# Windowed attention in pairs of blocks, with negated scores and four output tiles begun among the last ones

## The chip, the cores and the metric

The kernel runs on one core of a Trainium2 chip. The metric is the device time of one execution in microseconds (us). Before the change the median of three runs is 1871.75 us (1870.81 to 1874.26); the profile is of a further execution.

## The reference

An encoder of two layers on two sequences, a prompt of 256 rows and a sample of 512, with model width 1024, in fp32. Layer l=0 mixes rows by a gated recurrence (mLSTM), layer l=1 by windowed attention, and behind each mixer stands a gated FFN with a convolution of width 3. Only the attention is touched: 16 heads of 64 share 4 key/value heads; a block of 128 queries sees up to 384 keys (its own block and one on each side), and each head has a sink that counts in the denominator alone.

```python
s = jnp.einsum('bqkgd,bckd->bkgqc', qb, kb).astype(jnp.float32) * scale + bias
s = jnp.where(valid, s, -jnp.inf)
m = jnp.maximum(jnp.max(s, axis=-1, keepdims=True), sink_l)
p = jnp.exp(s - m)
denom = jnp.sum(p, axis=-1, keepdims=True) + jnp.exp(sink_l - m)
ob = jnp.einsum('bkgqc,bckd->bqkgd', p / denom, vb.astype(jnp.float32))
```

The result goes through an output projection, x = x + g1 * (ob @ w_out), and then into the FFN.

## The kernel before

Everything lies transposed, features on the 128 partitions and the 768 rows of both sequences along the free axis. A product of fp32 precision is made of three matmuls in a reduced format: each operand is split into a high part (a cast on ScalarE, `whi` or `zh`) and the rest (a subtraction on VectorE, `wlo` or `zl`), and PE computes hi by hi, lo by hi and hi by lo (L230). Weights come in loads of 512 KB into five buffers `raw`, and `split` puts them into `whi` and `wlo`, which rotate over three buffers each. An instruction that writes into a rotating buffer waits until the readers of its last content are done.

The attention is in `swa`. First keys and values are projected, then come the blocks: 8 head pairs j, for each the sample's four blocks and the prompt's two, 48 in all. `scores` makes for both heads e of the pair two matmuls into one of four PSUM banks `pa`, adds the bias and takes the maximum in one VectorE instruction (L1092), joins the sink by three small VectorE instructions (L1097 to L1099), takes the exponential with its row sum on ScalarE (L1101), that of the sink (L1104), adds, inverts (L1105, L1106) and scales on POOL (L1108). `flip` transposes the block on PE (L1116) and copies it out of PSUM, one head by ScalarE and one by VectorE. `values` multiplies by v into a bank `ps`, and behind a sequence's last block ScalarE copies the bank out (L1137); `pack` splits that once more for the projection. The query projections of the next head pairs are a generator, `project`, each of whose steps is three matmuls.

The order of PE is written out by hand (manual_schedule): per block a few steps of `project`, the scores of block x, the transposes of block x - 3, and after each third block the values of three blocks. Other engines run in the order in which their instructions are written, and so do the DMA issues on SP.

`out_proj` computes 16 tiles of 128 features by 384 rows, 24 matmuls each, and adds each to x on VectorE (L719, the residual). It is a generator over `tiles()`, which fetches and splits a tile's weights when it is advanced. It yields ahead of tile 8 and ahead of tile 15, the last. Between these yields `prepare` splits some of the FFN's first weights; what follows the second is `head`, which loads the four halves of the first FFN weights, writes the splits wa[0], the subtractions of `sums(0)` (L1390 to L1395 on VectorE) and the split wc[0], and only then runs the last tile. Then come the norm's row sums, the matmul on `nr`, the squared sum's power, which POOL works out, and the FFN's own products. For l=0 `prepare` splits three weights ahead, for l=1 one; the other two splits (128x1024) are in the head.

## Time and profile before

| what | us |
|---|---|
| median of three runs | 1871.75 |
| the profiled execution | 1875.08 |
| its span | 1873.0 |
| PE busy in the span | 1801.3 |
| VectorE busy | 1400.9 |
| attention blocks, first to last matmul | 1100.2 to 1257.8 |
| output projection of l=1 | 1257.8 to 1327.6 |

A busy time says only that an instruction was under way on the engine. The chain of waits and the timeline give in brackets for how long an engine was idle before an instruction, and whose end released it; the windows give busy times by stage, with the clock that was granted to PE.

### The profile page before, as it was taken

What the parts mean: (1) busy time and instruction counts of PE and PEld (TensorE: products, weight loads), DVE (VectorE), ACT (ScalarE), POOL (GpSimd) and SP (SyncE); (2) the same over time, 40 slices, a digit from 0 to 9 for tenths busy, and PEclk for the clock granted to TensorE, in tenths of its full rate; (3) what the DMA queues carried; (4) which work ended last, traced back from release to release, by engine and by line L of the source; (5) the groups of instructions that cost most, each with busy time, mean ns of one, the idle gap of its engine ahead of it and who ended that gap; (6) DMA issues with size and microseconds to landing.
All of it is one profiled execution on the core that took longest, in us unless ns stands there. A gap on an engine that the chain in (4) does not pass through costs nothing. (4 is left out here: it accounts for less than half of the span.)

```text
span 1873.0 us, 29153 instructions
## 1 busy us (share of the span) xinstructions
PE 1801.3 (96%) x11306; PEld 1662.3 (89%) x11306; DVE 1400.9 (75%) x2306; ACT 911.0 (49%) x1841; POOL 497.9 (27%) x390
## 2 busy tenths in 40 slices
PE   6989999999999999999999999989999999999997
PEld 5968887878988999999999898879989999999996
DVE  4866567685689777777777768875997777777777
ACT  4544334444455444444444556763565444444443
POOL 2011001031024333333331313330134333333322
PEclk9999999999999999999999999999999999999999
DMA  8353466555212222222222221212222222222211
GB/s 325 108 165 134 152 197 205 162 167 193 97 50 74 68 68 68 68 68 68 68 68 82 101 90 41 89 55 90 79 79 79 68 68 68 68 68 68 68 35 68
DMA packets 64246, 184.49 MB, mean 99 GB/s; under 512 B 6167, under 2 KB 23831, under 8 KB 64108
## 3 DMA queue, kind: packets, MB, share of 16 engines
q1 hardware_dynamic: 64108, 182.63, 30.1%
q8 instruction: 89, 1.46, 0.3%
q14 instruction: 49, 0.40, 0.1%
HBM read 176.17 MB, written 6.43 MB: 97 GB/s over the span
## 5 line engine op out<-in xcount | busy, mean ns | idle before, releaser
L236 ACT CAST whi<-raw 128x1024 fp32r<-128x1024 f32 x237 | 249.0, 1051 | 389.9 <-PE pa L230 198.6
L237 DVE TENSOR_TENSOR wlo<-raw,whi 128x1024 fp32r<-128x1024 f32 x237 | 316.3, 1335 | 108.8 <-ACT whi L236 107.7
L230 PE MATMUL pa<-slab,whi 128*128 128x256 f32 (+1 forms) x1472 | 346.9, 333 | 6.2 <-DVE slab L719 6.2
L230 PEld LDWEIGHTS pa<-slab,whi 128*128 128x128 f32 x1472 | 253.2, 190 | 33.1 <-DVE slab L719 7.1
L719 DVE SCALAR_TENSOR_TENSOR slab<-pa,mod,slab 128x256 f32<-128x256 f32 (+1 forms) x368 | 207.5, 591 | 70.9 <-PE pa L230 70.6
L230 PE MATMUL ps<-zh,whi 128*128 128x256 f32 (+2 forms) x688 | 233.4, 340 | 6.3 <-ACT whi L236 2.6
L230 PE MATMUL pa<-slab,wlo 128*128 128x256 f32 (+1 forms) x736 | 234.9, 331 | 0.0
L230 PE MATMUL ps<-zh,wlo 128*128 128x256 f32 (+2 forms) x688 | 228.3, 334 | 3.8 <-DVE wlo L237 3.8
L230 PE MATMUL ps<-zl,whi 128*128 128x256 f32 (+2 forms) x688 | 228.7, 334 | 1.4 <-DVE zl L539 0.9
L1275 PE MATMUL ps<-zh,whi 128*128 128x384 f32 x504 | 171.0, 339 | 6.4 <-ACT ps L1330 5.4
L1276 PE MATMUL ps<-zl,whi 128*128 128x384 f32 x504 | 169.7, 337 | 0.8 <-DVE zl L1233 0.8
L1277 PE MATMUL ps<-zh,wlo 128*128 128x384 f32 x504 | 169.0, 335 | 0.0
L230 PEld LDWEIGHTS pa<-slab,wlo 128*128 128x128 f32 x736 | 139.3, 190 | 12.9 <-DVE wlo L237 0.9
L230 PEld LDWEIGHTS ps<-zh,whi 128*128 128x128 f32 x688 | 132.2, 192 | 20.3 <-issue 3.5
L230 PEld LDWEIGHTS ps<-zh,wlo 128*128 128x128 f32 x688 | 132.2, 192 | 14.6 <-DVE wlo L237 4.6
L230 PEld LDWEIGHTS ps<-zl,whi 128*128 128x128 f32 x688 | 132.3, 192 | 10.7 <-DVE zl L539 1.1
L1531 POOL TENSOR_TENSOR slab<-slab 128x772 f32<-128x772 f32 x44 | 87.4, 1987 | 190.3 <-DVE slab L1503 178.9
L1306 POOL TENSOR_TENSOR raw<-raw,raw 128x512 f32<-128x512 f32 x40 | 53.7, 1341 | 291.7 <-DVE wlo L237 243.8
L1502 DVE SCALAR_TENSOR_TENSOR slab<-slab,cstt,slab 128x771 f32<-128x771 f32 x88 | 106.2, 1208 | 25.4 <-ACT slab L1500 25.4
L1503 DVE SCALAR_TENSOR_TENSOR slab<-slab,cstt,slab 128x771 f32<-128x771 f32 x88 | 120.1, 1365 | 0.8
L1303 POOL TENSOR_TENSOR raw<-raw 128x512 f32<-128x512 f32 x40 | 64.8, 1619 | 186.1 <-DMA raw<-in_w_dram 178.4
L472 DVE SCALAR_TENSOR_TENSOR ada<-raw,silc,ada 128x1024 f32<-128x1024 f32 x84 | 111.5, 1358 | 2.6 <-DMA raw<-in_adaln_w_dram 2.6
(300 smaller groups left out, 4163.8 us busy)
## 6 DMA issues: line engine op xcount, KB each, us to landing
raw<-in_w_dram SPq DMA_DIRECT2D x208, 512.0 KB, 3.7
raw<-in_adaln_w_dram SPq DMA_DIRECT2D x84, 512.0 KB, 4.5
slab<-in_x_dram SPq DMA_DIRECT2D x12, 512.0 KB, 7.7
slab<-in_adaln_w_dram SPq DMA_DIRECT2D x12, 512.0 KB, 10.3
slab<-mrows SPq DMA_DIRECT2D x8, 384.0 KB, 6.0
xs<-slab SPq DMA_DIRECT2D x6, 512.0 KB, 2.9
bt<-brow SPq DMA_DIRECT2D x16, 192.0 KB, 3.2
slab<-xs SPq DMA_DIRECT2D x6, 512.0 KB, 5.7
```

The lines of the kernel that those rows point to most:

```text
L230: self.last_mm = self.nc.tensor.matmul(out, lhsT, rhs, start=start, stop=stop)
L236: nc.scalar.copy(hi, src)
L237: return nc.vector.tensor_tensor(lo, src, hi.bitcast(F32), ALU.subtract)
L472: stt(acc[:, s], row, w, acc[:, s], ALU.mult, ALU.add)
L719: self.nc.vector.scalar_tensor_tensor(x, o, self.mod[l][:, gc + c, q : q + 1], x, ALU.mult, ALU.add)
L1275: mm(o, wh[:, k], hi[k], start=start and k == 0, stop=False, skip_group_check=True)
L1276: mm(o, wh[:, k], lo[k], start=False, stop=False, skip_group_check=True)
L1277: mm(o, wl[:, k], hi[k], start=False, stop=k == 3, skip_group_check=True)
L1303: tt(q[2], q[2], q[3], ALU.add)
L1502: stt(y[:, 1:], u[:, :-1], w(0), y[:, 1:], ALU.mult, ALU.add)
L1503: stt(y[:, :-1], u[:, 1:], w(2), y[:, :-1], ALU.mult, ALU.add)
L1531: nc.gpsimd.tensor_tensor(y, y, yrow[:, j], ALU.mult)
```

## The change

Scores are negated: queries are scaled by -0.125 and the bias changes sign, so that the minimum, begun at the negated sink, serves as the exponential's bias with a scale of -1. POOL copies the sink into the column behind the keys, so that the row sum holds it. Blocks go in 24 pairs. The transposes lag by one pair, and the values of three pairs, a whole head pair, come in one burst. Their result is split straight out of PSUM. For the last head pair the prompt's blocks come first. `out_proj` becomes the class `Out`: tiles 0 and 1 run six of their eight k steps among pairs 20 to 23, their seventh and tile 2 behind, then they are closed (residual and square), and the last value matmuls, tile 2 and tile 3 follow; `rest` does the other twelve. x is loaded when the last scores have been computed. `prepare` is the same for both layers.

```diff
-    def out_proj(self, u0, act, xt, l, apply):
-        def tiles():
-            kept = []
+    class Out:
+        def __init__(self, net, u0, act, l, xt):
...
+            self.count = 0
+        def tiles(self, u0):
+            net, kept = self.net, []
             for u in range(4):
-                for h, w in self.halves(u0 + u):
+                for h, w in net.halves(u0 + u):
                     kept.append(w)
                     yield 0, 2 * u + h, w
             for c in (5, 6, 7):
                 yield 1, c, kept[c]
-            yield 1, 4, self.split(self.load(u0 + 2, 0))
+            yield 1, 4, net.split(net.load(u0 + 2, 0))
             for u in range(2):
-                for h, w in self.halves(u0 + u):
+                for h, w in net.halves(u0 + u):
                     yield 1, 2 * u + h, w
-        norms = [Norm(self, xt, half, apply, last=True, adds=self.nc.vector) for half in HALVES]
-        self.turn = 1
-        for i, (z, c, w) in enumerate(tiles()):
-            if i in (KC, 2 * KC - 1):
-                yield
+        def open(self, bank):
+            _, (z, c, w) = next(self.todo)
             c0, c1, _ = HALVES[z]
-            o = self.ps()[:, : c1 - c0]
-            self.product(o, w, act, c0, c1)
-            self.tick(4.2)
+            return z, c, w, bank()[:, : c1 - c0]
+        def close(self, tile):
+            net = self.net
+            z, c, _, o = tile
+            c0, c1, _ = HALVES[z]
+            if self.norms is None:
+                apply = net.combined(self.l, 1)
+                self.norms = [Norm(net, self.xt, half, apply, last=True, adds=net.nc.vector) for half in HALVES]
             for p0, p1, q in pieces(c0, c1):
-                self.resid(xt, o[:, p0 - c0 : p1 - c0], l, 16, c, (p0, p1, q))
-            norms[z].square(c)
-            if i % KC == KC - 1:
-                self.start(HALVES[z], norms[z].stages())
-    def product(self, o, w, act, c0, c1):
+                net.resid(self.xt, o[:, p0 - c0 : p1 - c0], self.l, 16, c, (p0, p1, q))
+            self.norms[z].square(c)
+            self.count += 1
+            if self.count % KC == 0:
+                net.start(HALVES[z], self.norms[z].stages())
+        def rest(self):
+            net = self.net
+            net.turn = 1 + self.count
+            while self.count < 2 * KC:
+                if self.count in (KC, 2 * KC - 1):
+                    yield
+                tile = self.open(net.ps)
+                z, _, w, o = tile
+                net.product(o, w, self.act, *HALVES[z][:2])
+                net.tick(4.2)
+                self.close(tile)
+    def product(self, o, w, act, c0, c1, ks=range(KC)):
...
+        nc.vector.tensor_scalar(nsk, self.cst(SK, 16), -1.0, None, ALU.mult)
...
-                    nc.scalar.activation(hi, src, AF.Copy, scale=0.125)
-                    nc.vector.scalar_tensor_tensor(lo, src, 0.125, hi.bitcast(F32), ALU.mult, ALU.subtract)
...
+                    nc.scalar.activation(hi, src, AF.Copy, scale=-0.125)
+                    nc.vector.scalar_tensor_tensor(lo, src, -0.125, hi.bitcast(F32), ALU.mult, ALU.subtract)
...
+        out = self.Out(self, U_AOUT, lambda k, s0, s1: [att[k // 2][:, z, k % 2, s0:s1] for z in range(2)], 1, None)
...
+        begun = []
+        def part(i, k):
+            z, _, w, o = begun[i]
+            self.product(o, w, out.act, *HALVES[z][:2], (k,))
...
-        def pack(c):
-            for s0, s1 in SEQS:
-                self.fp_copy_split(self.hh[:, c, s0:s1], self.hl[:, c, s0:s1], att[c // 4][:, c % 4, s0:s1])
+        def begin():
+            for i in range(2):
+                begun.append(out.open(self.ps))
+                for k in range(6):
+                    part(i, k)
+                    yield
...
-            for q, (s0, s1) in enumerate(SEQS):
+            for q, (s0, s1) in enumerate(SEQS) if j < 7 else ((1, SEQS[1]), (0, SEQS[0])):
...
-                    bt = pool.tile([P, 384], F32, tag="bt", name=self.nm("bt"), bufs=3)
+                    bt = pool.tile([P, 384], F32, tag="bt", name=self.nm("bt"), bufs=4)
...
-            b.t = t = pool.tile([P, 2, 384], F32, tag="t", name=self.nm("t"), bufs=4)
...
+            sk = nsk[:, 2 * j : 2 * j + 2]
+            b.t = t = pool.tile([P, 2, 388], F32, tag="t", name=self.nm("t"), bufs=4)
...
+            nc.gpsimd.tensor_copy(t[:, :, K : K + 1], sk.unsqueeze(2))
+            S = [self.pa()[:, :K] for _ in range(2)]
             for e in range(2):
-                S = self.pa()[:, :K]
-                qb = qts[j // 2][:, 2 * (j % 2) + e, q0 : q0 + P]
                 for z in range(2):
-                    self.mm(S, qb, kk[kv // 2][:, kv % 2, z, k0 : k0 + K], z == 0, z == 1)
+                    self.mm(
+                        S[e], qts[j // 2][:, j % 2, e, q0 : q0 + P], kk[kv // 2][:, kv % 2, z, k0 : k0 + K],
+                        z == 0, z == 1,
+                    )
+            for e in range(2):
                 nc.vector.tensor_tensor_reduce(
-                    out=t[:, e, :K], in0=S, in1=bias[j][e][:, 384 - co - K : 384 - co][:, ::-1], op0=ALU.add, op1=ALU.max,
-                    scale=1.0, scalar=-BIG, accum_out=rm[:, e : e + 1],
+                    out=t[:, e, :K], in0=S[e], in1=bias[j][e][:, 384 - co - K : 384 - co][:, ::-1], op0=ALU.add, op1=ALU.min,
+                    scale=1.0, scalar=sk[:, e : e + 1], accum_out=mn[:, e : e + 1],
                 )
-            sk = self.cst(SK + 2 * j, 2)
-            nc.vector.tensor_tensor(mx, rm, sk, ALU.max)
-            nc.vector.tensor_tensor(rd, sk, mx, ALU.subtract)
-            nc.vector.tensor_scalar(mx, mx, -1.0, None, ALU.mult)
             for e in range(2):
                 nc.scalar.activation(
-                    t[:, e, :K], t[:, e, :K], AF.Exp, bias=mx[:, e : e + 1], accum_out=sm[:, e : e + 1]
+                    t[:, e, : K + 1], t[:, e, : K + 1], AF.Exp, bias=mn[:, e : e + 1], scale=-1.0,
+                    accum_out=sm[:, e : e + 1],
                 )
-            nc.scalar.activation(rd, rd, AF.Exp)
-            nc.vector.tensor_tensor(rd, rd, sm, ALU.add)
-            nc.vector.reciprocal(rd, rd)
+            nc.vector.reciprocal(rd, sm)
...
+            if turn % 18 < 8:
+                return self.tmp([P, 384])
+            return pool.tile([P, 384], F32, tag="pt", name=self.nm("pt"), bufs=10)
         def flip(b):
-            b.pt = pool.tile([P, 2, 384], F32, tag="pt", name=self.nm("pt"), bufs=5)
+            b.pt = [turned() for _ in range(2)]
...
+        def pack(b, c0, c1):
...
+            self.fp_copy_split(
+                att[u][:, 0, c, s0 + c0 : s0 + c1], att[u][:, 1, c, s0 + c0 : s0 + c1], po[b.j, b.q][:, c0:c1]
+            )
...
-            if b.i == b.n - 1:
-                nc.scalar.copy(att[j // 4][:, j % 4, b.s0 : b.s1], o[:, : b.s1 - b.s0])
+            if j == 7 and b.q == 0:
+                if b.i == 0:
+                    pack(b, 0, P)
+                elif b.i == b.n - 1:
+                    pack(b, P, b.n * P)
+            elif b.i == b.n - 1:
+                pack(b, 0, b.n * P)
         fill = project()
...
+        first = begin()
+        pairs = [blocks[x : x + 2] for x in range(0, len(blocks), 2)]
+        np_ = len(pairs)
+        done = 0
...
+        def feed(upto):
+            nonlocal done
+            while done < min(total, upto):
+                next(fill, None)
+                done += 1
+            if done == total:
+                next(fill, None)
         with self.tc.manual_schedule(engines={mybir.EngineType.PE}):
-            for x in range(nb + LAG + 1):
-                while done < min(113, AHEAD + (x + 1) * (113 - AHEAD) // 40):
-                    next(fill, None)
-                    done += 1
-                if x < nb:
-                    scores(blocks[x])
-                if LAG <= x < nb + LAG:
-                    flip(blocks[x - LAG])
-                if x > LAG and (x - LAG) % GROUP == 0:
-                    for b in blocks[x - LAG - GROUP : x - LAG]:
+            for p in range(np_ + 2):
+                for b in pairs[p] if p < np_ else ():
+                    scores(b)
+                if p < 20:
+                    feed(8 + (8 * p + 5) * (total - 8) // 157)
+                elif p < 24:
+                    self.step(first, 2)
+                if p == np_:
+                    drain(first)
+                    part(0, 6)
+                    part(1, 6)
+                for b in pairs[p - 1] if 1 <= p <= np_ else ():
+                    flip(b)
+                if p == np_:
+                    group = pairs[p - 3 : p - 1]
+                elif p == np_ + 1:
+                    group = pairs[p - 2 : p - 1]
+                else:
+                    group = pairs[p - 4 : p - 1] if p % 3 == 1 and p > 3 else ()
+                for pair in group:
+                    for b in pair:
                         values(b)
-                    if x >= 36 and b.i == b.n - 1 and b.q == 1:
-                        while packed <= b.j:
-                            pack(packed)
-                            packed += 1
-        return None
+                if p < 20:
+                    feed(8 + (8 * p + 8) * (total - 8) // 157)
+                elif p < 24:
+                    self.step(first, 1)
+                if p == np_:
+                    out.xt = self.load_x(xs, (PROMPT,) + RANGES[:2])
+                    begun.append(out.open(self.pa))
+                    for k in range(KC - 1):
+                        part(2, k)
+                    for i in range(2):
+                        part(i, 7)
+                        out.close(begun[i])
+            part(2, 7)
+            out.close(begun[2])
+            begun.append(out.open(self.pa))
+            for k in range(KC):
+                part(3, k)
+            out.close(begun[3])
+        return out
...
         self.fp_copy_split(*wa, self.load(u0 + 1, 0))
-        for i in range(0 if l else 2):
+        for i in range(2):
             self.fp_copy_split(*ahead[i], self.load(u0 + 3 + i, 0))
...
-        if not done:
-            self.fp_copy_split(*ahead[0], ah[0])
...
-        if not done:
-            self.fp_copy_split(*ahead[1], ah[1])
...
+                last_tile = out.rest()
                 next(last_tile)
```

On PE, at the end of the attention before: score matmuls (`pa` from two slabs), transposes (`pa` from `kct` and `t`) and values (`ps` from `pt` and `vn`).

```order
L230 MATMUL pa_12495<-slab_9917,slab_11706 128x256 x2
L230 MATMUL pa_12499<-slab_9917,slab_11706 128x256 x2
L1116 MATMUL pa_12514<-kct,t_12387 128x128 x3
L1116 MATMUL pa_12519<-kct,t_12387 128x128 x3
L230 MATMUL pa_12526<-slab_9917,slab_11706 128x256 x2
L230 MATMUL pa_12530<-slab_9917,slab_11706 128x256 x2
L1116 MATMUL pa_12545<-kct,t_12416 128x128 x3
L1116 MATMUL pa_12550<-kct,t_12416 128x128 x3
L1116 MATMUL pa_12556<-kct,t_12445 128x128 x2
L1116 MATMUL pa_12560<-kct,t_12445 128x128 x2
L230 MATMUL ps_12564<-pt_12465,vn 64x128 x4
L230 MATMUL ps_12564<-pt_12513,vn 64x128 x6
```

The same stretch now, pair 23: `ps_12328` is output tile 1.

```order
L224 MATMUL pa_12396<-slab_9919,slab_11641 128x384 x2
L224 MATMUL pa_12397<-slab_9919,slab_11641 128x384 x2
L224 MATMUL pa_12412<-slab_9919,slab_11641 128x256 x2
L224 MATMUL pa_12413<-slab_9919,slab_11641 128x256 x2
L224 MATMUL ps_12328<-slab_11355,whi_12324 128x384 x2
L224 MATMUL ps_12328<-slab_11355,wlo_12325 128x384
L224 MATMUL ps_12328<-slab_11881,whi_12324 128x384 x2
L224 MATMUL ps_12328<-slab_11881,wlo_12325 128x384
L1157 MATMUL pa_12433<-kct,t_12290 128x128 x2
L1157 MATMUL pa_12437<-kct,t_12290 128x128 x2
L1157 MATMUL pa_12443<-kct,t_12306 128x128 x3
L1157 MATMUL pa_12448<-kct,t_12306 128x128 x3
```

The blocks stood alone; now matmuls of the output projection stand between scores and transposes, which go by two blocks and follow their scores by one pair.

On VectorE, around the last output tile of l=1, before: `wlo_13217` is that tile's split, `ps_12627` and `ps_12624` are the residuals of tiles 13 and 14, `wlo_13247` is wa[0], `wlo_13257` wc[0].

```order
L237 TENSOR_TENSOR wlo_13217<-raw_13214,whi_13216 128x1024
L719 SCALAR_TENSOR_TENSOR slab_12633<-ps_12627,mod_89,slab_12633 128x384
L112 TENSOR_TENSOR nt_12961<-nt_12961,nt_13144 128x384
L237 TENSOR_TENSOR wlo_13247<-raw_13228,whi_13246 128x1024
L1390 TENSOR_TENSOR raw_13230<-raw_13230 128x512
L112 TENSOR_TENSOR nt_12961<-nt_12961,nt_13178 128x384
L719 SCALAR_TENSOR_TENSOR slab_12633<-ps_12624,mod_89,slab_12633 128x384
L1392 TENSOR_TENSOR raw_13228<-raw_13230,raw_13228 128x512
L1393 TENSOR_TENSOR raw_13228<-raw_13228 128x512
L1394 TENSOR_TENSOR s1l_13227<-raw_13230,s1h_13226 128x512
L1395 TENSOR_TENSOR raw_13230<-raw_13230,raw_13228 128x512
L237 TENSOR_TENSOR wlo_13257<-raw_13228,whi_13256 128x1024
```

Now: `ps_12621` and `ps_12622` are the residuals of tiles 14 and 15, `wlo_13105` is wc[0], `wlo_13111` the last tile's split.

```order
L1476 TENSOR_TENSOR raw_13080<-raw_13082,raw_13080 128x512
L106 TENSOR_TENSOR nt_12818<-nt_12818,nt_13035 128x384
L1477 TENSOR_TENSOR raw_13080<-raw_13080 128x512
L1478 TENSOR_TENSOR s1l_13079<-raw_13082,s1h_13078 128x512
L713 SCALAR_TENSOR_TENSOR slab_12508<-ps_12621,mod_89,slab_12508 128x384
L1479 TENSOR_TENSOR raw_13082<-raw_13082,raw_13080 128x512
L231 TENSOR_TENSOR wlo_13105<-raw_13080,whi_13104 128x1024
L231 TENSOR_TENSOR wlo_13111<-raw_13108,whi_13110 128x1024
L713 SCALAR_TENSOR_TENSOR slab_12508<-ps_12622,mod_89,slab_12508 128x384
```

The last tile's split stood ahead of tile 13's residual and now stands behind tile 14's residual and wc[0], directly ahead of its own tile's residual. The cast into `whi_13110` moves on ScalarE in the same way, behind that of wc[0]. The order for l=0 is alike.

More of the change, by code (lines that the diff above doesn't have):

```diff
@@ L35 @@
 EPS = 1e-6
-LAG = 3
-GROUP = 3
-AHEAD = 6
 HELD = float("inf")
@@ L1026, in swa @@
         self.gemmN(U_AIN + 1, lambda t, o: nc.scalar.copy(v[:, t], o))
-        att = [self.slab([P, 4, T]) for _ in range(2)]
+        att = [None] * 4
+        out = self.Out(self, U_AOUT, lambda k, s0, s1: [att[k // 2][:, z, k % 2, s0:s1] for z in range(2)], 1, None)
         def weights():
@@ L1352, in prepare @@
         wa = place(0)
-        spare = None
-        if l:
-            spare = self.slab([P, 3072], R)
-            wa = [spare[:, 1024 * (z + 1) : 1024 * (z + 2)] for z in range(2)]
         self.fp_copy_split(*wa, self.load(u0 + 1, 0))
-        for i in range(0 if l else 2):
+        for i in range(2):
             self.fp_copy_split(*ahead[i], self.load(u0 + 3 + i, 0))
-        return wa, ahead, spare
+        return wa, ahead
     def head(self, u0, last_tile, pool, urows, mark, early):
@@ L1367, in head @@
         part = lambda w, i: [t[:, 512 * i : 512 * (i + 1)] for t in w]
-        wa2, ahead, spare = early
-        done = spare is None
-        spare = spare or self.slab([P, 3072], R)
+        wa2, ahead = early
+        spare = self.slab([P, 3072], R)
         s1 = [
@@ L1378, in head @@
         ra[1], rb[1] = (self.load(u0 + 1, h) for h in range(2))
-        ah = [None if done else self.load(u0 + 3 + i, 0) for i in range(2)]
         q = [[t[:, 512 * i : 512 * (i + 1)] for t in ab for i in range(2)] for ab in zip(ra, rb)]
```

65 lines of the change are left out of this document (40 added, 25 removed).

## The prediction

> **What bounds the kernel now.** I read the page's engine shares first. The profiled execution took 1875.08 us, and its span is 1873.0 us (2.1 lie around it).
>
> ```profile
> span 1873.0 us, 29153 instructions
> PE 1801.3 (96%) x11306; PEld 1662.3 (89%) x11306; DVE 1400.9 (75%) x2306; ACT 911.0 (49%) x1841; POOL 497.9 (27%) x390
> ```
>
> PE sets the end, so an edit is worth what it takes out of PE's stalls. A view by stage shows where those are; the attention blocks run from 1100 to 1257.8, the output projection from there to 1327.6, the head of the FFN of l=1 behind it.
>
> ```profile
> 1104.00:1124.00 20.00, 18.50 (x131) 16.09 (x131) 14.60 (x68) 13.80 (x41) 5.10 (x10) 1.00 0.24 76
> 1143.00:1162.00 19.00, 19.00 (x162) 16.89 (x160) 15.52 (x66) 13.31 (x43) 6.06 (x12) 1.00 0.17 50
> ...
> 1219.00:1238.00 19.00, 15.87 (x130) 13.73 (x127) 16.71 (x72) 15.86 (x53) 6.94 (x12) 0.86 0.34 103
> 1238.00:1258.00 20.00, 17.49 (x173) 13.66 (x172) 13.83 (x68) 13.64 (x47) 8.45 (x18) 0.97 0.01 3
> 1258.00:1329.00 71.00, 71.00 (x419) 71.00 (x419) 43.44 (x78) 30.78 (x57) 0.87 (x1) 1.00 0.27 83
> 1329.00:1390.00 61.00, 55.35 (x310) 51.62 (x309) 59.07 (x76) 38.75 (x72) 21.36 (x12) 1.00 0.24 77
> ```
>
> The first figure after the length is PE's busy time, the last but two the granted clock. The blocks idle at their end (15.87 of 19), where the clock also falls to 0.86; the projection has no idle PE at all; in the head VectorE has 59.07 of 61.
>
> A busy PE is not yet a dense one, so I took the step from one start to the next out of the timeline.
>
> ```profile
> 1150.00 1.53 PE L230 MATMUL ps<-pt,vn 128*64 128x128 f32 x24
> 1151.46 0.50 PE L230 MATMUL ps<-zh,whi 128*128 128x512 f32 x1
> 1151.80 0.39 PE L230 MATMUL ps<-zl,whi 128*128 128x512 f32 x1
> 1152.03 0.39 PE L230 MATMUL ps<-zh,wlo 128*128 128x512 f32 x1
> ...
> 1153.64 0.64 PE L230 MATMUL pa<-slab,slab 128*128 128x256 f32 x4
> 1154.11 0.82 PE L1116 MATMUL pa<-kct,t 128*128 128x128 f32 x6
> ...
> 1155.00 0.40 PE L230 MATMUL ps<-zl,whi 128*128 128x512 f32 x1
> ```
>
> A 128x512 matmul steps 0.23 (1151.80 to 1152.03), four score matmuls take 0.47 (0.118 each). Six transposes and one 128x512 take 0.89 (1154.11 to 1155.00): (0.89 - 0.23) / 6 = 0.11 each. A burst of 24 value matmuls with one 128x512 takes 1.80, 1.57 without it. Counts come from the groups of 1104 to 1258.
>
> ```profile
> L230 PE MATMUL ps<-zh,whi 128*128 128x512 f32 x51 | 21.7, 425 | 0.0
> L230 PE MATMUL ps<-zh,whi 128*128 128x256 f32 x56 | 17.4, 310 | 0.0
> L230 PE MATMUL pa<-slab,slab 128*128 128x256 f32 x128 | 22.9, 299 | 0.0
> L230 PE MATMUL pa<-slab,slab 128*128 128x384 f32 x64 | 14.5, 347 | 1.1 <-DVE st L1092 1.0
> L1116 PE MATMUL pa<-kct,t 128*128 128x128 f32 x224 | 37.0, 289 | 6.2 <-DVE st L1099 2.4 <-POOL t L1108 1.3 <-DVE st L1097 1.2
> L230 PE MATMUL ps<-pt,vn 128*64 128x128 f32 x448 | 28.3, 278 | 0.0
> ```
>
> The first two rows stand for three groups each (hi by hi, lo by hi, hi by lo). A value matmul streams 128 columns, for which I take a quarter of the 128x512's step, 0.057; a 128x384 takes 0.174 (26 of them from 1323.05 to 1327.57, quoted below). So 153 x 0.23 + 168 x 0.118 + 128 x 0.118 + 64 x 0.174 + 224 x 0.11 + 448 x 0.057 = 35.2 + 19.8 + 15.1 + 11.1 + 24.6 + 25.5 = 131.3 us of work in 154. **22.7 us** are stalls and switches. A value burst's switch is 1.57 - 24 x 0.057 = 0.20.
>
> **Part by part: the attention.** The matmuls stay, in other company. Where the 22.7 us lie in the tail is shown by these rows (idle before and its releaser in brackets).
>
> ```profile
> 1227.90 0.74 PE L1116 MATMUL pa<-kct,t 128*128 128x128 f32 x4 [0.38 <-DVE st L1092]
> ...
> 1233.16 1.12 PE L1116 MATMUL pa<-kct,t 128*128 128x128 f32 x4 [2.39 <-DVE st L1099]
> ...
> 1257.80 0.44 PE L230 MATMUL ps<-zh,whi 128*128 128x384 f32 x1 [0.73 <-ACT slab L1137]
> ```
>
> In 1219 to 1258 the query projections are used up and PE has only the blocks' own chain. In the changed kernel 36 matmuls of output tiles 0 and 1 stand there, tile 2 behind the last transposes. Cut per block are four small VectorE operations, of which the first row is one, and one exponential of ScalarE:
>
> ```profile
> L1098 DVE TENSOR_TENSOR st<-cstt,st 128x2 f32<-128x2 f32 x48 | 11.4, 237 | 0.8
> ...
> L1104 ACT ACTIVATE st<-st 128x2 f32<-128x2 f32 x48 | 9.7, 203 | 23.3 <-DVE st L1098 22.9
> ```
>
> Four of about 0.2 us in 48 blocks are some 38 us of VectorE beside PE's work: worth nothing by themselves, but they shorten the chain that ends in waits like that of 2.39. The POOL copy of 128x2 added per block has no row; operations of that size take about 0.2 on the two other engines (the rows above). It stands ahead of the scores, so I take 0 for it; 0.2 on the chain of each of the last four pairs' blocks would be 1.6 us. That a wait for the x load holds up tile 0's residual costs nothing in my reading: the loads are issued at the last scores, and PE has tile 2 (about 4 us) and the flips and values (about 4) before the first residual needs them.
>
> What stays of the 22.7: nine value bursts, now sixteen, at 0.20 and a little more for longer queues in front of the copies (2.2); the start, whose lack is the 1.50 of 1104 to 1124 (1.5); pairs 20 to 23, where the transposes follow their scores by one pair alone and the row of 0.38 is what a wait of this kind costs (4 x 0.4 = 1.6); the last flip and tile 3's split, which is queued behind four residuals (1.2); and one and a half switches of 0.1 in each of 24 pairs (1151.46 to 1151.80 is 0.34 where 0.23 is the step): 3.6. Together 10.1; half and one and a half times the waits in it put the ends at 8 and 14. **Gain 12.6** (8.7 to 14.7), of which 3.3 is the half clock at 1232.6.
>
> **The last output tile of both layers.** This is the term that decides. Before, the loop over the weights fetches and splits the last tile's pair before it yields, so this split stands ahead of the head. Now the generator yields first, and load, cast and split are written in the head's order, behind those of wa[0] and wc[0]. The pair of buffers it gets is the one tile 14 reads. So its cast starts when tile 14 ends, and its split stands on VectorE behind tile 14's residual, one subtraction and wc[0]'s split. Durations from before, with X the end of tile 14 (1323.05):
>
> ```profile
> 1323.05 0.52 PE L230 MATMUL ps<-yh 128*128 128x384 f32 x2
> ...
> 1327.57 0.34 PE L1275 MATMUL ps<-yh,whi 128*128 128x384 f32 x1
> ```
> ```profile
> 1323.25 0.62 DVE L719 SCALAR_TENSOR_TENSOR slab<-ps,mod,slab 128x384 f32<-128x384 f32 x1 [0.79 <-PE ps L230]
> 1323.79 0.68 DVE L1392 TENSOR_TENSOR raw<-raw,raw 128x512 f32<-128x512 f32 x1
> ...
> 1326.44 1.22 DVE L237 TENSOR_TENSOR wlo<-raw,whi 128x1024 fp32r<-128x1024 f32 x1
> ```
>
> The residual starts at X + 0.20 and the next at X + 0.74; the subtraction takes 0.6 to its successor, a split 1.14 to the next and 1.22 to its end: X + 0.74 + 0.6 + 1.14 + 1.22 = X + 3.7. The third matmul of tile 15, due at X + 0.35, needs it: **3.4 us late**, in two pieces (cast, then split). The same order stands in l=0, so 6.8 in all. Nothing else is ready for PE in its queue.
>
> Before has one place of this shape, and the clock falls there:
>
> ```profile
> 404.91 0.50 PE L230 MATMUL ps<-zh,whi 128*128 128x512 f32 x1 [1.41 <-ACT whi L236]
> ...
> 407.30 0.80 PE L230 MATMUL ps<-zh,wlo 128*128 128x512 f32 x1 [1.41 <-DVE wlo L237]
> ```
> ```profile
> 408.00:410.00 2.00, 2.00 (x6) 1.55 (x5) 2.00 (x4) 1.05 (x1) 0.00 (x0) 0.50 0.82 281
> ```
> ```profile
> 607.75 0.51 PE L230 MATMUL pa<-slab,whi 128*128 128x256 f32 x2 [1.70 <-DVE slab L719]
> ```
> ```profile
> 608.00:610.00 2.00, 2.00 (x17) 2.00 (x17) 2.00 (x5) 0.65 (x1) 0.00 (x0) 1.00 0.04 8
> ```
>
> Two waits of 1.41 in 3.8 us halve it (0.50), one of 1.70 alone doesn't (1.00), one of 2.39 at 1233.16 does (the 0.86 above). Mine are about 1.4 and 1.7 within 3.6 us, nearest to the first. The half clock at 1233 holds the window 1219 to 1238 to 0.86 and the next to 0.97: 19 x 0.14 + 20 x 0.03 = 3.3 us lost. I take 3.2 a head, with a chance of 0.8 for each head (both 0.64, one 0.32).
>
> [...]
>
> **The heads.** For l=1 two splits of 1.23 leave VectorE's queue, and POOL's late result at l=0 should go, since the loads in front of it now land earlier against the stalled PE.
>
> ```profile
> 516.44 0.34 PE L1275 MATMUL ps<-yh,whi 128*128 128x384 f32 x1
> ...
> 523.48 0.71 PE L230 MATMUL pa<-kct,nr 128*128 128x128 f32 x4 [0.69 <-POOL nr L131]
> ...
> 567.17 0.44 PE L1275 MATMUL ps<-zh,whi 128*128 128x384 f32 x1 [1.28 <-ACT ps L1330]
> ```
> ```profile
> 1379.15 0.44 PE L1275 MATMUL ps<-zh,whi 128*128 128x384 f32 x1 [1.30 <-ACT ps L1330]
> ```
>
> From the end of tile 15 to this row l=1 takes 1379.15 - 1327.57 = 51.6, and l=0, which has its weights split early already, 567.17 - 516.44 = 50.7 with the 0.69 in it. Now both should take 50.0: 0.7 + 1.6 = **2.3 gained**. The two 128x1024 splits themselves move into the projection, where VectorE has 43.44 of 71.
>
> **The sum.** Against the profiled execution: 1875.08 - 12.6 + 6.8 + 2 x 3.2 - 2.3 = 1873.4. That execution is 3.3 us above the median of 1871.75, the size of one half clock, which I take to have fallen by chance and out of an ordinary run: 1873.4 - 3.3 = 1870.1. A measurement of this kernel can tell about 0.2% (3.7 us) from no change.
>
> **The rivals.** (a) One drop, or none: 1870.1 - 3.2 = 1866.9 or 1863.7. [...] Chance 0.26, the rule's share of it 0.06.
> (b) No stall at tile 15, because its load and casts find more room than I read: 1870.1 - 6.8 - 6.4 = 1856.9. Against it stands the order of the split on VectorE, which no load changes. 0.09.
> (c) Slower: the scores of a pair take four PSUM banks and the transposes of the pair before four more, and a lag of one pair is too short for minimum, exponential, row sum and scaling of two blocks, so each flip waits. The row at 1227.90 shows that even a lag of three blocks waits 0.38 where the fill is thin; against it stand the 19.00 of 19.00 of 1143. Beyond what I counted, 0.4 us a pair over 24 pairs takes 9.6 us: 1879.7. From (1875.5 - 1870.1) / 24 = 0.23 a pair on it is slower. 0.12.
> (d) Pairs do less than said: a switch between transposes and matmuls is no cost to be saved (the step of 0.11 already holds it), the tail fills but the rest stays as it is, at the low end of the gain: 1870.1 + 12.6 - 8.7 = 1874.0. 0.09.
>
> **How the numbers follow.** Forecast (both stalls, both drops) 0.44, own range 1866 to 1874. Of it I count 0.16 as faster, 0.25 same, 0.03 slower. (a) gives 0.22 faster and 0.04 same, (b) 0.09 faster, (c) 0.12 slower, (d) 0.07 same and 0.02 slower: faster 0.47, same 0.36, slower 0.17. The range that leaves out most of (b) and (c) is 1860 to 1876.
>
> **What would show it.** Right: PE waits of about 1.4 and 1.7 us at the start of tile 15 in both layers, the first by the cast, the second by the split, and a granted clock of 0.50 behind them; no idle above 1 us in the last pairs; the projection's rest 12 tiles of 4.2; no wait for nr at l=0. Wrong: tile 15 starting without a wait; flips that wait in each pair; a wait of tile 0's residual for the x load; PE waiting in tile 3 longer than 2 us.

## The result, and the profile after

The changed kernel takes 1861.31 us (median of four, 1857.14 to 1862.33), the kernel before 1872.26 in the same comparison: ratio 0.9937, 95% interval 0.9922 to 0.9953. The forecast was 1870.1, a gain of 2 us; the gain is 11. The profiled execution took 1862.14 us, with a span of 1860.0.

The windows of the changed kernel (PE's busy time first, the granted clock last but two):

```profile
1104.00:1124.00 20.00, 19.90 (x130) 17.75 (x129) 13.34 (x43) 12.86 (x37) 7.97 (x20) 1.00 0.25 73
1143.00:1162.00 19.00, 18.82 (x159) 16.78 (x158) 13.75 (x44) 12.89 (x38) 7.52 (x18) 1.00 0.18 50
...
1219.00:1238.00 19.00, 19.00 (x202) 18.12 (x201) 14.36 (x50) 12.89 (x43) 9.83 (x24) 1.00 0.10 29
1238.00:1257.00 19.00, 18.31 (x148) 17.16 (x147) 10.70 (x28) 9.09 (x21) 2.08 (x4) 1.00 0.59 203
1257.00:1306.00 49.00, 49.00 (x290) 49.00 (x289) 34.03 (x64) 25.35 (x48) 0.86 (x1) 1.00 0.35 116
1306.00:1311.00 5.00, 2.39 (x12) 1.75 (x11) 3.56 (x5) 1.98 (x3) 0.00 (x0) 0.99 0.18 49
1311.00:1318.00 7.00, 7.00 (x35) 7.00 (x34) 2.29 (x3) 0.76 (x2) 4.44 (x5) 0.77 0.32 115
```

The end of the attention is dense (19.00 of 19 where 15.87 stood), and so is its start. The hole is now at 1306 to 1311, 2.39 of 5, with a clock of 0.77 behind it. The timeline names it, in both layers:

```profile
508.51 0.62 PE L224 MATMUL ps<-slab,whi 128*128 128x384 f32 x2 [0.90 <-ACT whi L230]
510.84 0.44 PE L224 MATMUL ps<-slab,wlo 128*128 128x384 f32 x1 [1.71 <-DVE wlo L231]
...
521.55 0.93 PE L224 MATMUL pa<-kct,nr 128*128 128x128 f32 x6 [0.40 <-POOL nr L125]
...
1245.33 0.88 PE L224 MATMUL ps<-nt,vn 128*64 128x128 f32 x12 [0.69 <-DVE slab L231]
...
1307.61 0.62 PE L224 MATMUL ps<-slab,whi 128*128 128x384 f32 x2 [0.88 <-ACT whi L230]
1309.96 0.45 PE L224 MATMUL ps<-slab,wlo 128*128 128x384 f32 x1 [1.73 <-DVE wlo L231]
```

These are the two waits foretold, at the first and the third matmul of the last output tile, first for the cast, then for the split. At l=0 the clock stays at 1.00 behind them:

```profile
512.00:520.00 8.00, 8.00 (x54) 8.00 (x54) 2.89 (x5) 2.02 (x5) 3.73 (x5) 1.00 0.26 91
```

From 1098 to 1306, the stretch of the blocks and most of the projection, PE waits for little that the waits view shows (line, releaser, us in total, times, longest):

```profile
PE ps L224 <- DVE slab L231: 0.7, 1, 0.7
PE pa L1157 <- DVE st L1129: 0.3, 2, 0.2
```

The two waits of the second row stand at 1125.63 and 1144.48, where query projections still fill PE; in the last pairs the view shows none ahead of the transposes.

For the experiments I measure stretches on PE, each in the one profiled execution of its kernel: the output projection of l=0 (its first matmul to the first FFN matmul), and for l=1 blocks with projection (the last value-projection matmul to the first FFN matmul). "Half clock" is the time in the second stretch for which the clock was granted at half (0.50); half of it is counted as lost, an estimate from that figure. Measured in the changed kernel: the last 21 matmuls of tile 15 take 5.23 at l=1, with 3.4 of half clock among them (1310.25 to 1315.48), and 3.69 at l=0 (511.12 to 514.81), 1.54 less. "Chain" is the mean time of a block, from the start of its first extreme (maximum or minimum) to the end of its second scaling, blocks 4 to 39 (counted from 0). "Head" in the text is the time from a layer's first FFN matmul to the matmul behind ScalarE's copy, the one at 567.17 and 1379.15 in the prediction's rows.

| kernel | projection l=0 | blocks and projection l=1 | half clock in it | chain | median us |
|---|---|---|---|---|---|
| before | 70.57 | 227.47 | 6.8 | 6.56 | 1872.26 |
| after | 73.76 | 216.73 | 3.4 | 4.08 | 1861.31 |
| e1_fetch_first | 70.60 | 212.01 | 0 | 4.08 | 1855.74 |
| e2_late_before | 73.76 | 227.35 | 3.4 | | 1874.45 |
| e3_no_tiles | 70.58 | 218.10 | 0 | 4.08 | 1863.75 |
| e4_short_bursts | 70.57 | 215.06 | 0 | | 1858.64 |
| e5_old_sign | 70.60 | 231.69 | 6.8 | 6.57 | 1873.36 |
| e6_old_prepare | 70.58 | 212.05 | 0 | | 1856.63 |
| e7_sign_alone | 70.57 | 217.45 | 0 | 4.17 | 1860.54 |
| e8_same_pair | 70.60 | 229.19 | 3.4 | 3.71 | 1874.17 |
| e9_off_chain | 70.58 | 213.20 | 0 | 4.21 | 1856.97 |
| e10_old_sign_lag2 | 70.60 | 217.85 | 0 | 6.16 | 1859.35 |
| e11_after_again | 73.74 | 215.07 | 0 | | 1860.60 |
| e12_fetch_again | 70.59 | 211.99 | 0 | | 1856.53 |

One of the ten executions of e8_same_pair took 4159.23 us and is left out of its ratio.

### The profile page after: what moved, and what is told of

It is laid out like the page before. It is cut to its first block, busy times and chain, and to the rows that moved or that the text cites. A ratio compares the mean times of both kernels' runs of the same rounds, so it can differ in the third digit from the quotient of the medians.

```text
span 1860.0 us, 28918 instructions
## 1 busy us (share of the span) xinstructions
PE 1789.5 (96%) x11306; PEld 1657.0 (89%) x11306; DVE 1377.7 (74%) x2116; ACT 898.3 (48%) x1778; POOL 507.6 (27%) x438
## 5 line engine op out<-in xcount | busy, mean ns | idle before, releaser
L224 PE MATMUL pa<-slab,whi 128*128 128x256 f32 (+2 forms) x1504 | 355.9, 333 | 6.1 <-DVE slab L713 6.1
L713 DVE SCALAR_TENSOR_TENSOR slab<-pa,mod,slab 128x256 f32<-128x256 f32 (+2 forms) x372 | 209.0, 590 | 70.5 <-PE pa L224 70.2
L224 PE MATMUL pa<-slab,wlo 128*128 128x256 f32 (+2 forms) x752 | 240.6, 331 | 0.0
L224 PE MATMUL ps<-zh,whi 128*128 128x256 f32 (+1 forms) x560 | 187.2, 335 | 6.3 <-ACT whi L230 2.6
L224 PE MATMUL ps<-zh,wlo 128*128 128x256 f32 (+1 forms) x560 | 183.7, 330 | 3.4 <-DVE wlo L231 3.4
L224 PE MATMUL ps<-zl,whi 128*128 128x256 f32 (+1 forms) x560 | 184.6, 331 | 1.3 <-DVE zl L533 0.9
L224 PE MATMUL ps<-slab,whi 128*128 128x384 f32 x480 | 125.1, 342 | 2.3 <-ACT whi L230 1.8
L224 PEld LDWEIGHTS ps<-zh,whi 128*128 128x128 f32 x560 | 106.7, 191 | 18.7 <-ACT whi L230 3.2
L224 PEld LDWEIGHTS ps<-zh,wlo 128*128 128x128 f32 x560 | 106.9, 191 | 14.0 <-DVE wlo L231 4.2
L224 PEld LDWEIGHTS ps<-zl,whi 128*128 128x128 f32 x560 | 106.9, 191 | 10.3 <-DVE zl L533 1.1
```

The source lines that it names most:

```text
L224: self.last_mm = self.nc.tensor.matmul(out, lhsT, rhs, start=start, stop=stop)
L713: self.nc.vector.scalar_tensor_tensor(x, o, self.mod[l][:, gc + c, q : q + 1], x, ALU.mult, ALU.add)
```

## The experiments

**The last tile.** The first kernel fetches the weights ahead of the yield again.

```diff
...
                 if self.count in (KC, 2 * KC - 1):
+                    self.held.append(next(self.todo))
                     yield
...
-            _, (z, c, w) = next(self.todo)
+            _, (z, c, w) = self.held.pop() if self.held else next(self.todo)
```

> The changed kernel, with the last output tile's weights fetched and split ahead of the head again, in both layers. Theory (PE loses what it waits at tile 15, 3.3 us in each layer, and what the clock loses behind it): no wait at tile 15 in l=0 or l=1, no half clock there, 1861.3 - 6.6 - 1.7 = 1853.0, from 1851 to 1856. Rival (the head is bound by VectorE, which works on through PE's wait, so that the time comes back by the end of the head): 1860 to 1862, and the stretch from the end of tile 14 to the matmul behind L1421's copy as long as with the wait.

Measured: 1855.74 us, ratio to before 0.9918 (0.9903 to 0.9933). Both stretches fall, by 3.16 and 4.72. The heads behind them give 1.0 us of that back (50.57 and 50.66, where the changed kernel has 50.45 and 49.78). PE's waits from 1100 to 1315 are down to these, the second of them in the head:

```profile
PE ps L224 <- DVE slab L231: 0.7, 1, 0.7
PE pa L224 <- POOL nr L125: 0.6, 1, 0.6
PE pa L1159 <- DVE st L1131: 0.4, 2, 0.2
```

The second is the same fault alone, put into the kernel before at l=0.

```diff
-        for i, (z, c, w) in enumerate(tiles()):
-            if i in (KC, 2 * KC - 1):
+        todo = tiles()
+        for i in range(2 * KC):
+            if i == KC or l == 0 and i == 2 * KC - 1:
                 yield
+            z, c, w = next(todo)
+            if l == 1 and i == 2 * KC - 1:
+                yield
```

> The kernel before, with the fetch and split of the last output tile put behind the yield in l=0 alone. Theory (the wait costs its own length wherever it stands): PE waits of about 0.9 and 1.7 us at tile 15 of l=0, 3.3 us in all, 1872.3 + 3.3 = 1875.6; 1877 to 1879 where the clock falls as well. Rival (covered by VectorE's work in the head): 1872.3, unchanged.

Measured: 1874.45 against 1871.27 of the kernel before, ratio 1.0020 (1.0008 to 1.0032), so 3.2 us or 1.5 to 6.0; the stretch of l=0 is 3.19 longer, as in the changed kernel. In its stretch the wait costs its length, 3.19 for the 3.3 expected. The head behind gives only 0.6 of it back (50.13, where 50.73 stood): the wait of 0.69 for `nr` is gone there.

The last two repeat both on one chip, without a change.

> The changed kernel as it is, on one chip with e12_fetch_again. [...] Rival for the clock (the place decides, as the first profile had it at l=1 and not at l=0): again at l=1 alone.

> e1_fetch_first once more beside e11_after_again. Theory (6.2 us of waits less 1 that the heads give back, and 1 to 2 of clock): 5 to 8 us below e11_after_again, 1854 to 1857. Rival (the waits are mostly given back): within 2 us of it.

Measured: 1860.60 (ratio 0.9952, 0.9937 to 0.9968) and 1856.53 (0.9918, 0.9904 to 0.9932). The intervals don't overlap, so the kernel with the fetch ahead is faster than both kernels of this case. The gap of 4.1 is below the 5 to 8 that were expected, and below the 5.2 that waits of 6.2 less the heads' 1.0 leave. In e11_after_again the waits are the same to 0.01 us, and the clock falls at neither place (1.00 from 505 to 515 at l=0, and at l=1 as below):

```profile
1305.54 0.62 PE L224 MATMUL ps<-slab,whi 128*128 128x384 f32 x2 [0.88 <-ACT whi L230]
1307.90 0.45 PE L224 MATMUL ps<-slab,wlo 128*128 128x384 f32 x1 [1.73 <-DVE wlo L231]
```
```profile
1308.00:1315.00 7.00, 7.00 (x44) 7.00 (x45) 2.88 (x3) 1.00 (x2) 3.16 (x5) 1.00 0.43 143
```

So neither the place nor the waits' length settles it.

**The tiles and the bursts.** All further kernels but e7_sign_alone stand on e1_fetch_first.

```diff
-                elif p < 24:
-                    self.step(first, 2)
-                if p == np_:
-                    drain(first)
-                    part(0, 6)
-                    part(1, 6)
...
                     out.xt = self.load_x(xs, (PROMPT,) + RANGES[:2])
-                    begun.append(out.open(self.pa))
...
-            part(2, 7)
-            out.close(begun[2])
...
-            out.close(begun[3])
```

> Like e1_fetch_first, but none of the output tiles is begun among the last blocks; all 16 follow the attention. Theory (the tiles fill what the blocks' own chain leaves idle): in each of pairs 20 to 23 and behind the last one PE waits 1 to 3 us for the chain of minimum, exponential and scaling, 8 to 12 us in all with a half clock among them, 1861 to 1866. Rival (the shorter chain and the pairs alone ended the waits): at most 2 us more than e1_fetch_first, 1853 to 1856.

Measured: 1863.75 (0.9955, 0.9942 to 0.9968), the stretch 6.1 longer. The time is as expected, its form is not: the waits on the timeline are small and no half clock is among them.

```profile
1220.79 1.07 PE L1159 MATMUL pa<-kct,t 128*128 128x128 f32 x7 [0.22 <-DVE st L1131]
1221.62 1.51 PE L224 MATMUL pa<-slab,slab 128*128 128x256 f32 x8
1222.97 1.76 PE L1159 MATMUL pa<-kct,t 128*128 128x128 f32 x8
1224.48 1.74 PE L224 MATMUL pa<-slab,slab 128*128 128x256 f32 x8
1226.06 1.55 PE L1159 MATMUL pa<-kct,t 128*128 128x128 f32 x8
...
1234.96 1.94 PE L1159 MATMUL pa<-kct,t 128*128 128x128 f32 x10 [0.74 <-POOL t L1142]
...
1242.20 0.62 PE L224 MATMUL ps<-slab,whi 128*128 128x384 f32 x2 [1.17 <-DVE slab L231]
```

Eight score matmuls take 1.35 and 1.58 here (1221.62 to 1222.97, 1224.48 to 1226.06) where 8 x 0.118 = 0.94 is their work, and eight transposes 1.51 (1222.97 to 1224.48) where 8 x 0.11 = 0.88 is. So gaps between matmuls of one group count as busy. The idle time that the view shows is only 2.5 us more than in e1_fetch_first; the other 3.6 of the 6.1 lie in such gaps.

```diff
-                if p == np_:
-                    group = pairs[p - 3 : p - 1]
-                elif p == np_ + 1:
-                    group = pairs[p - 2 : p - 1]
-                else:
-                    group = pairs[p - 4 : p - 1] if p % 3 == 1 and p > 3 else ()
+                group = pairs[p - 2 : p - 1] if p > 1 else ()
```

> Like e1_fetch_first, but values of one pair in each burst, 24 bursts in place of 9. Theory (each burst costs a switch of 0.20 to 0.30 us): 15 more switches, 3 to 4.5 us, 1856 to 1858. Rival (a switch is free, or earlier values free buffers and gain as much): within 1 us of e1_fetch_first.

Measured: 1858.64 (0.9938, 0.9922 to 0.9953), just above the expected times, the stretch 3.05 longer: 3.05 / 15 = 0.20 for each burst, the figure that the prediction took from one row.

**The sign.** In the next kernel the scores have their old sign, in the pairs.

```diff
...
-            nc.gpsimd.tensor_copy(t[:, :, K : K + 1], sk.unsqueeze(2))
...
-                    scale=1.0, scalar=sk[:, e : e + 1], accum_out=mn[:, e : e + 1],
+                    scale=1.0, scalar=-BIG, accum_out=rm[:, e : e + 1],
...
+            nc.vector.tensor_tensor(mx, rm, sk, ALU.max)
+            nc.vector.tensor_tensor(rd, sk, mx, ALU.subtract)
+            nc.vector.tensor_scalar(mx, mx, -1.0, None, ALU.mult)
...
+            nc.scalar.activation(rd, rd, AF.Exp)
+            nc.vector.tensor_tensor(rd, rd, sm, ALU.add)
...
```

> Like e1_fetch_first, but with the scores' old sign: the four small VectorE operations and the exponential of the sink are back in each block, the POOL copy is out. Measured on PE's stretch from the last value-projection matmul to the end of the output projection (212.0 us in e1_fetch_first, 227.5 before). Theory (these operations are hidden beside PE as long as there is fill, and a lag of one pair has room for them): at most 213, 1855 to 1857. Rival (the pairs' short lag only holds because the chain got shorter by about 1 us): waits ahead of the transposes in most pairs, 0.3 to 0.5 us each, 219 to 224, 1863 to 1868.

Measured: 1873.36 (1.0006, 0.9994 to 1.0018). The whole gain is gone; the stretch is 231.69, 19.7 longer, of which 3.4 is counted for the half clock. My theory is refuted, and the rival (219 to 224) was still too small. PE's waits in it:

```profile
PE pa L1162 <- POOL t L1145: 11.2, 8, 2.5
PE pa L224 <- DVE st L1129: 1.4, 4, 0.5
```

The converse is the new sign alone in the kernel before, with the minimum, the POOL copy and the exponential as in the change and all else as before.

> The kernel before with the negated scores and the sink in the row sum alone; blocks, bursts, projection as before. Theory (the small operations matter only where the fill has run out, at the end): the stretch from the last value-projection matmul to the end of the output projection falls from 227.5 by 2 to 5 us, mostly by the wait of 2.4 and the half clock behind it, 1867 to 1870. Rival (hidden there too): 226.5 to 227.5, 1871 to 1872.

Measured: 1860.54 (0.9935, 0.9915 to 0.9956), and a stretch 10.0 shorter, 3.4 of that counted for the half clock. That is twice what the theory allowed (2 to 5), and not at the end alone. From the first maximum of block 4 to that of block 36 the kernel before takes 102.7 us for 819 matmuls, and the new sign 98.9 for as many:

```profile
1115.60:1218.30 102.70, 101.71 (x819) 89.41 (x817) 84.75 (x349) 72.85 (x234) 34.51 (x66) 1.00 0.23 70
```
```profile
1107.20:1206.10 98.90, 98.86 (x819) 88.80 (x817) 70.04 (x224) 69.17 (x205) 43.71 (x98) 1.00 0.24 73
```

Only 1.0 us of the 3.8 shows as idle PE; the rest are gaps that count as busy. The sign alone brings as much as the whole change does with its fault. Why shows in one block of the kernel before, on VectorE:

```profile
1154.18 0.42 DVE L1092 CUSTOM_DVE_ANT_0 t<-pa,bt 128x256 f32<-128x256 f32 x1 [0.28 <-PE pa L230]
...
1154.76 0.42 DVE L1092 CUSTOM_DVE_ANT_0 t<-pa,bt 128x256 f32<-128x256 f32 x1
...
1155.18 0.54 DVE L1118 COPY pt<-pa 128x384 f32<-128x384 f32 x1
1155.64 0.31 DVE L1097 TENSOR_TENSOR st<-st,cstt 128x2 f32<-128x2 f32 x1
1155.98 0.42 DVE L1098 TENSOR_TENSOR st<-cstt,st 128x2 f32<-128x2 f32 x1
1156.44 0.17 DVE L1099 TENSOR_SCALAR st<-st 128x2 f32<-128x2 f32 x1
1157.37 0.42 DVE L1092 CUSTOM_DVE_ANT_0 t<-pa,bt 128x256 f32<-128x256 f32 x1 [0.76 <-PE pa L230]
...
1157.83 0.16 DVE L1105 TENSOR_TENSOR st<-st 128x2 f32<-128x2 f32 x1
1157.91 0.42 DVE L1092 CUSTOM_DVE_ANT_0 t<-pa,bt 128x256 f32<-128x256 f32 x1
...
1158.25 0.16 DVE L1106 RECIPROCAL st<-st 128x2 f32<-128x2 f32 x1
```

and on ScalarE:

```profile
1156.44 0.21 ACT L1104 ACTIVATE st<-st 128x2 f32<-128x2 f32 x1 [1.27 <-DVE st L1098]
1156.70 0.51 ACT L1101 ACTIVATE t<-t,st 128x256 f32<-128x256 f32 x1
```

The second maximum is through by 1155.2, but the first exponential starts at 1156.70: a copy and three small operations stand between, one behind the other. The sum (L1105) and the reciprocal (L1106) then stand behind the next block's two maxima: the sum ends at 1157.99, but the reciprocal starts at 1158.25, when the second maximum is nearly through. With the new sign alone, on the same two engines:

```profile
1154.20 0.62 DVE L1096 CUSTOM_DVE_ANT_0 t<-pa,bt,nsk 128x384 f32<-128x384 f32 x1 [0.32 <-POOL t L1107]
1154.74 0.61 DVE L1096 CUSTOM_DVE_ANT_0 t<-pa,bt,nsk 128x384 f32<-128x384 f32 x1
...
1156.28 0.17 DVE L1105 RECIPROCAL st<-st 128x2 f32<-128x2 f32 x1 [0.58 <-ACT t L1101]
```
```profile
1154.94 0.62 ACT L1101 ACTIVATE t<-t,st 128x385 f32<-128x385 f32 x1
```

Here the first exponential starts 0.1 us after the first minimum's end (1154.82), beside the second minimum. Is it the chain, or the engines' time? Two kernels tell that apart. One gives the work back, where nobody waits for it:

```diff
...
             nc.vector.reciprocal(rd, sm)
+            nc.scalar.activation(sx[:, 0:2], sk, AF.Exp)
+            nc.vector.tensor_tensor(sx[:, 2:4], mn, sk, ALU.max)
+            nc.vector.tensor_tensor(sx[:, 2:4], sk, mn, ALU.subtract)
+            nc.vector.tensor_scalar(sx[:, 2:4], mn, -1.0, None, ALU.mult)
+            nc.vector.tensor_tensor(sx[:, 2:4], mn, sm, ALU.add)
```

> Like e1_fetch_first, with four small VectorE operations of 128x2 and a small exponential added to each block again, written behind the reciprocal and read by nobody (their results are not used; the computation is else the same). Theory (what counts is the chain from scores to scaled block, 4.1 us with the new sign and 6.6 with the old one, and not the engines' work): the stretch from the last value-projection matmul to the end of the output projection 212 to 214, 1856 to 1858. Rival (the work in the queues of VectorE and ScalarE): towards the 231.7 of e5_old_sign, over 222.

Measured: 1856.97 (0.9914, 0.9889 to 0.9940), stretch 213.20, 1.2 more than without, as the theory had it. The other keeps the long chain and gives it room, with six score buffers in place of four and fewer for the transposed blocks:

```diff
...
-                for b in pairs[p - 1] if 1 <= p <= np_ else ():
+                for b in pairs[p - 2] if 2 <= p <= np_ + 1 else ():
...
```

> Like e5_old_sign (old sign on e1_fetch_first), but with transposes two pairs behind their scores (six score buffers, fewer for the transposed blocks). Theory (the long chain of 6.6 us only misses a lag of one pair): the waits on POOL's scaling vanish from the fill's part, the stretch falls from 231.7 to 214 to 219, 1858 to 1863. Rival (the old sign's ping-pong between VectorE and ScalarE bounds the pairs whatever the lag): over 226, 1869 and more.

Measured: 1859.35 (0.9929, 0.9912 to 0.9946), stretch 217.85, as the theory had it, although the chain still takes 6.16. Work off the chain costs 1.2 of e5_old_sign's 19.7; room for the chain gives 13.8 of them back, 3.4 of that counted for the half clock. So in the pairs it is the chain against the lag. The sizes fit: in e1_fetch_first blocks 4 to 36 take 99.0 us, 6.2 a pair; a chain of 4.08 has room in a lag of one pair, and one of 6.57 has not. Of the 5.8 that e10_old_sign_lag2 still loses, its waits view shows 2.3 ahead of scores, behind a maximum, and 2.9 behind the copies of transposed blocks. For the kernel before, with its lag of three blocks (3 x 3.2 us), nothing but the new sign was tried.

The lag the other way: transposes behind their own pair's fill, by moving the same loop behind the second feed, with `pairs[p]`.

> Like e1_fetch_first, but the transposes of a pair stand behind the fill of its own pair, a lag of the fill alone (about 3.9 us to pair 19, 1.6 in pairs 20 to 23). Theory (the chain from the last score to the scaled block takes about 3.7 us, as pair 23 of the changed kernel shows, which waits nowhere): waits of 0 to 0.5 us in pairs 0 to 19 and of about 2 us in the last four, the stretch 212 + 8 to 18 = 220 to 230. Rival (the chain takes 5 us or more when ScalarE and VectorE have the fill's evacuations in front): over 1.2 us in each pair, 240 and more.

Measured: 1874.17 (1.0011, 0.9998 to 1.0025), stretch 229.19 with 1.7 counted for a half clock, within the theory's range but not in its form. Ten waits for the scaling sum to 9.3; seven of them, 0.9 to 2.2 each and 8.0 in all, stand where there is still fill, and the last four pairs, which were to wait about 2 us each, wait 1.3 together:

```profile
PE pa L1159 <- POOL t L1142: 9.3, 10, 2.2
```

**The splits in the head.** e6_old_prepare has for l=1 the old `prepare`, and the two splits in the head.

```diff
-        for i in range(2):
+        for i in range(0 if l else 2):
             self.fp_copy_split(*ahead[i], self.load(u0 + 3 + i, 0))
...
```

> Like e1_fetch_first, but with the old order of the FFN's weights for l=1: two splits of 128x1024 stand in the head again. Theory (they lie on VectorE's queue in a head that VectorE bounds): the head of l=1 takes 51.6 us as before, where it takes 50.7 in e1_fetch_first, 0.9 more, 1856.6. Rival (worth the whole 1.6 forecast): 52.3. Rival (nothing): 50.7.

Measured: 1856.63 (0.9917, 0.9899 to 0.9934), not to be told from e1_fetch_first. A half clock of 6.8 us fell into the head of its profiled execution, so that the head's length (56.9 with it) decides nothing. Waits of 1.43 and 0.40 for ScalarE and 0.37 for VectorE, which e1_fetch_first's head has not, speak for a cost; the median does not show it. This is left open.

## Why the prediction was right or wrong

The time lies in the range, and faster was the likeliest of its three answers, but the forecast was 8.8 us too high. The measured time is outside the forecast's own range of 1866 to 1874 and 1.3 us above the lower end of the stated one, which takes in rival (a); that rival alone gives 1866.9 or 1863.7. To end inside was partly luck, for the two large errors have the same sign. By its steps:

- **The last output tile: right.** It named the cause, both places and the two pieces. The split came when it was foretold, 3.7 us behind X (1306.22 to 1309.96). Forecast 3.4 us each; measured 3.16 (73.76 - 70.60) at l=0 and 3.0 at l=1 (216.73 - 212.01, less the 1.7 counted for the half clock). The difference is a reading: with 26 matmuls of 0.174 from X on, the 24 of tile 15 begin at X + 0.35, so its third is due at X + 0.70. Rival (b), no stall, is out.
- **The clock: mis-sized.** The step was "3.2 a head, with a chance of 0.8 for each head". In the two profiled executions of the changed kernel the clock fell behind one of the four last tiles, and there for 3.4 us, counted as 1.7 (1.54 on the 21 matmuls); the 6.8 us in the trace of before count as 3.4. 6.4 was in the sum, 1.7 by this count was paid in the first execution and nothing in the second: the largest error, 4.7 us. Rival (a) was the better case. Of its chance of 0.26 a share of 0.06 stands on a rule that no run shows; the runs show a clock of 0.77 over 7 us behind the two waits in one execution and of 1.00 in another.
- **The attention: the sum too small, its reason wrong.** Forecast 12.6; measured 227.47 - 212.01 = 15.5, an error of 2.9. The step that failed is "worth nothing by themselves", of the small operations. It called the chain shorter and then priced it at nothing outside the tail. The sign alone gives 10.0 of the 15.5, 3.8 of them between blocks 4 and 36, and without it pairs lose 19.7 to e1_fetch_first. A row that hinted at it was there: L1104's 23.3 us of idle ScalarE, <-DVE st L1098, is the chain's hop through VectorE in 48 blocks, quoted for its busy time and not read for its wait.
- **The tiles and bursts: right; the pairs: no gain of their own.** The tiles give 6.1, a burst costs 0.20. From the kernel before over e7_sign_alone (217.45) and e3_no_tiles (218.10) to e1_fetch_first (212.01) the 15.5 fall into 10.0 for the sign, a loss of 0.65 for pairs, fewer bursts, the direct split and the new order of the last head pair together, and 6.1 for the tiles. The 7 bursts saved should give 1.4, so the rest of the middle step costs some 2 us; what does was not tested. In that rival (d), "Pairs do less than said", was right. With the old sign the pairs and the tiles together lose 4.2 (231.69 against 227.47).
- **Waits of pairs 20 to 23, and of tile 3's split: too dear.** 2.8 us were counted; the waits view shows none ahead of those transposes and 0.7 for the last split of a value bank. Tile 0's residual doesn't wait for x, as reasoned: VectorE idles 5.38 us ahead of it, to 1250.65, for PE's `ps`.
- **The heads: right in sum, not in its parts.** Forecast 2.3. l=0 takes 50.45 and l=1 49.78, where 50.73 and 51.58 stood: 2.1. But at l=0 `nr` still waits 0.40, and e1_fetch_first, where PE is on time, takes 50.57 and 50.66: 1.1 are the heads' own gain, and 1.0 hung on PE being late.
- **Rival (c), too short a lag,** did not happen, and the kernels show how near it stood: with the old chain of 6.6 us the same lag costs all of the gain.

The clock's 4.7, the attention's 2.9 and the last tile's 0.6, less 0.2 for the heads, are 8.0 of the 8.8.

The spans of the two profiled executions differ by 13.0 us (1873.0 and 1860.0). The stretches and heads account for all but 3.3 of it, and that is a half clock of 6.8 us at 406, which the trace of before has and that of after has not; the prediction's 3.3 for an ordinary run stands for it.

## What to carry to other kernels

Where PE is fed by a chain through other engines, measure that chain from its first to its last instruction and set it against the lag in PE's order; small operations on it count by the hops and by what stands ahead of them in each queue (here a chain of 6.57 us with them and of 4.08 without), and the same operations off it are nearly free (1.2 us here against 19.7). When a generator's yield is moved past a fetch, follow the fetch's cast, split and buffer into the new order: one line cost 3 us in each of two places. An idle engine's row can say in its wait what its busy time doesn't (L1104: 9.7 us busy, 23.3 idle ahead of it). And test the parts of a change one after the other: here one of them, the pairs, gave nothing without the tiles.

## What was not expected of the hardware

The granted clock does not follow from the kernel's place alone. The same two waits (0.88 and 1.73 us) were followed by a clock of 0.77 over 7 us in one execution and of 1.00 in another. The spread of the times goes with it: the ten executions of e11_after_again reach from 1857.47 us, at a mean clock of 0.994, to 1869.01, at 0.988, and 0.006 of 1860 us is 11. A half clock lasted 3.4 us at tile 15 of the changed kernel (1310.9 to 1314.3) and 6.8 at two places of the kernel before (406.5 to 413.4, 1232.6 to 1239.4). What decides between the two lengths, and whether these waits are followed by one at all, was not found. And matmuls that the timeline joins in one group can hide waits: e3_no_tiles lost 6.1 us, of which the waits view shows some 2.5 more than in e1_fetch_first.
